# Delta-rule stage: PSUM evictions moved to ScalarE, square roots by logarithm, engine queues tied to the recorded TensorE order, and a full-height rotary product

## The chip, the cores and the metric

The kernel runs on one core of a Trainium2 chip. The metric is device time in microseconds (us), the median of the runs; the profile is of one further execution. Engines are called as on the profile's page: PE (TensorE), PEld (its weight loads), DVE (VectorE), ACT (ScalarE), POOL (GpSimd), SP (SyncE, which issues the DMAs).

## What is computed

One layer of a gated encoder on two sequences (512 and 256 tokens, joined to 768 columns), width 2048. A wide input projection feeds two branches: a gated delta rule over 8 heads of 128 in both directions, and a latent attention over 8 heads. The two are gated, mixed and projected back. Cut to what matters here:

```
qkv = silu(depthwise_conv(proj_qkv));  q, k = l2norm(q), l2norm(k)          # 8 heads of 128
for each chunk (delta rule, forward and on the reversed sequence):
    a   = I + strict_lower((beta k) k^T * decay);   u, w = a^-1 [beta v, beta k exp(g)]
    v'  = u - w S;   o = (q exp(g)) S + lower(q k^T * decay) v'
    S   = S exp(g_last) + (k exp(g_last - g))^T v'
o_a = rmsnorm(o_fwd + o_bwd) * silu(gate_a)
o_b = softmax((q_nope k_nope^T + rot(q_pe) rot(k_pe)^T) / sqrt(192)) v * silu(gate_b)
y   = rmsnorm(x + (sigmoid(gm_a) * (o_a w_pa) + sigmoid(gm_b) * (o_b w_pb)) w_out)
```

Products that need precision are made of three products of halves: each float32 operand is split into a rounded high part and a low part, and high*high, high*low and low*high are summed in PSUM.

## The kernel before

A Python class records the program instruction by instruction. The order of PE's instructions is written out by a little clock: a main generator yields after each projection product, and tasks (generators that `spawn` starts) yield the model nanoseconds after which they want to go on; `run` lets a due task record its next piece between two products. A task's `yield 4000` therefore means "go on once PE has been given 4 us more of work, by the model's prices". PE keeps the recorded order. The queues of DVE, ACT and POOL are then made by the compiler's scheduler, which simulates the engines and puts an instruction into its engine's queue where its inputs are ready in that simulation. Each queue runs strictly in order on the chip. `here_on` ties one instruction behind the latest PE instruction recorded so far, without a semaphore.

The work has three phases. Phase 1 (to about 1400 us) is the input projection: first by a seven-product scheme (`seven`), which fills PE, then nine ordinary blocks (`OTHERS`, columns of `gm_b`), each scaled on DVE, put through a sigmoid on ACT and stored. Phase 2 is the latent projections, phase 3 the two branch projections and the output projection. Between the products of the nine ordinary blocks and of phase 2, about 1240 to 1800 us, the delta rule's tasks run, one head after the other, with the next head begun before the last one is done:

- `gdn_decays` makes the decay matrices E of a head: POOL multiplies masks with gates (`rh`), PE sums them, ACT takes exp, POOL masks. Four groups per head; the first three heads are made ahead.
- `gdn_front` turns k to tokens (`ktok`, PE transposes and a DVE copy), ACT sums squares (`ss`), DVE makes `cc`, PE makes k k^T and q^T k (`kq`), DVE makes U from them, ACT `qk`.
- `gdn_values` does the same sums for q, takes square roots (`sk`, `rq`), and scales the transposed v (`vs`).
- `gdn_blocks` inverts the 32 by 32 diagonal blocks on DVE: 31 steps of two instructions (`spare`, `Y`), then a transpose into `spare`. `gdn_place` copies the result into X and W, half of the copies on ACT, half on DVE.
- `gdn_merge` joins blocks in small PE products with evictions between them (`q1s`, X and W, `q2s`, X).
- `gdn_chain`, four at a time (two sequences, two directions), walks the chunks: PE, then `r` (DVE) and `t` (ACT), PE, then `vn`, PE, then the state S, E (ACT) and an addition (POOL).
- `gdn_end` adds the directions, sums squares on ACT (`junk`, `so`), takes the root, inverts it into `f`, and scales.

Four PSUM buffers (`aps`) serve all of these, and the scores of attention too. On ACT a function that the loaded table set lacks is preceded by an `ACT_TABLE_LOAD`.

In attention the rotary part of the scores uses `qpe`, whose first 64 rows hold the high part and whose last 64 the low part, and `kpe[0]` and `kpe[1]`, the high and low part of the rotated keys, the same in both halves of the rows.

Of the kernel before, what the change touches and what calls it, by code (L numbers as in the profile page):

```python
# [53 lines left out]

class Layer:
# [4 lines left out]
    def __init__(self, tc, a):  # L60
        self.tc, self.nc, self.a = tc, tc.nc, a
        self.es = ExitStack()
# [573 lines left out]
    def gdn_decays(self, s):  # L636

        nc, gp, h = self.nc, self.gp, s["h"]
        E = s["E"] = gp.tile([P, 2, NCH, P], F32, name="E", bufs=3)
        for d in range(2):  # L640
            mask = self.minc[d].unsqueeze(1).broadcast_to([P, 3, P])
            for g0 in (0, 3):
                parts = []
                for src in (self.ghi, self.glo):
                    rh = gp.tile([P, 3, P], F32R, name="rh", tag="rh", bufs=3)
                    nc.gpsimd.tensor_tensor(rh, mask, src[:, g0:g0 + 3, d * 8 + h].bitcast(F32).unsqueeze(2).broadcast_to([P, 3, P]), op=ALU.mult)
                    parts.append(rh)
                yield 4000
                ps = self.apsum()
                for i in range(2):  # L650
# [7 lines left out]
    def gdn_front(self, s):  # L658
        nc, gp, h, kq = self.nc, self.gp, s["h"], s["kq"]
# [4 lines left out]
        for c0, n, ps in self.tposed(kT):  # L664
            nc.vector.tensor_copy(ktok[:, c0:c0 + n, :], ps)
# [27 lines left out]
    def gdn_values(self, s):  # L693

        nc, gp = self.nc, self.gp
# [6 lines left out]
        nc.scalar.activation(sk, ss, AF.Sqrt, bias=self.eps)  # L702
        s["rq"] = small("rq", [NCH])
        nc.vector.reciprocal(s["rq"], sk[:, 1, :])
# [10 lines left out]
    def gdn_blocks(self, s):  # L715


        nc, gp = self.nc, self.gp
# [26 lines left out]
    def gdn_place(self, s, R):  # L745

        nc, X, W = self.nc, self.X, self.W
# [11 lines left out]
    def gdn_merge(self, s, d):  # L759

        nc, gp, U, X, W = self.nc, self.gp, s["U"][:, d], self.X[d], self.W[d]
# [20 lines left out]
        for p in range(2):  # L782
            A, B = src(p), dst(p)
            nc.vector.tensor_scalar(X[A, :, B], x1[A, :192].rearrange("p (n c) -> p n c", c=32), -1.0, None, op0=ALU.mult)
            if p == d:
                nc.vector.tensor_scalar(W[B, :, wc], x1[B, 192:384].rearrange("p (n c) -> p n c", c=32), -1.0, None, op0=ALU.mult)
# [6 lines left out]
        nc.vector.tensor_copy(q2s[B], q2[B, :384].rearrange("p (n c) -> p n c", c=64))  # L793
# [4 lines left out]
        nc.vector.tensor_scalar(X[A, :, B], x2[A, :384].rearrange("p (n c) -> p n c", c=64), -1.0, None, op0=ALU.mult)  # L798
# [6 lines left out]
    def gdn_chain(self, s, q, d):  # L805
        nc, gp, h, o = self.nc, self.gp, s["h"], s["E"][:, d]
        chunks = SEQS[q] if d == 0 else SEQS[q][::-1]
        S = None
        for step, n in enumerate(chunks):
# [16 lines left out]
            nc.vector.tensor_scalar(vn, p2[:, 0:P], s["cc" if first else "ncc"][:, d, n:n + 1], None, op0=ALU.mult)  # L826
# [8 lines left out]
            if not last:  # L835
                new = gp.tile([P, P], F32, name=f"S{q}{d}", bufs=2 - q)
                if first:
                    nc.vector.tensor_copy(new, p3[:, P:2 * P])
# [12 lines left out]

    def gdn_end(self, s):
        nc, gp = self.nc, self.gp
# [8 lines left out]
        nc.scalar.activation(so, so, AF.Sqrt, bias=self.eps, scale=1.0 / P)  # L862
        f = gp.tile([P, NCH], F32, name="f", bufs=2)
        nc.vector.reciprocal(f, so)
# [64 lines left out]
    def phase1(self):  # L929
# [16 lines left out]
        for i, t in enumerate(OTHERS):  # L946
# [3 lines left out]
            nc.scalar.activation(f, f, AF.Sigmoid)  # L950
# [130 lines left out]
    def attention(self):  # L1081
# [20 lines left out]
        def scores(u):  # L1102
# [3 lines left out]
            for i in range(2):  # L1106
# [4 lines left out]
                self.mm(s, qpe[h][:64, qs], kpe[1][:64, keys], start=False, stop=True)  # L1111
# [74 lines left out]
    def phase3(self):  # L1186
# [47 lines left out]
        def mixed(j, i, g, pa):  # L1234
            def done(f):
                x = raws[j][i]
                nc.vector.tensor_tensor(g, f, g, op=ALU.mult)
# [304 lines left out]
```

## Time and profile before

| | |
|---|---|
| median of 3 runs (lowest, highest) | 2547.22 us (2547.01, 2550.58) |
| the profiled execution | 2548.74 us |
| its span, first to last instruction | 2547.0 us |
| PE busy | 2430.3 us (95%) |
| DVE busy | 1960.1 us (77%) |
| ACT busy | 1112.6 us (44%) |
| POOL busy | 539.1 us (21%) |
| mean granted clock of PE | 0.975 of full speed |

A busy PE means that a matmul was in flight; matmuls overlap, so the distance from one start to the next is shorter than one matmul's duration. The page's 40 slices show PE at nine tenths or more nearly everywhere; the lower digits stand at the start, from about 1280 to 1730 us, around 2110 to 2310 us and in the last slice. The granted clock is below nine tenths in slices near 1300, and near the end.

### The profile page before, as it was taken

The numbers are of one execution on the slowest core, as the hardware profiler recorded it, in microseconds if no ns is written. First come the engines' busy times: TensorE is split into PE (matmuls) and PEld (weight loads), VectorE is DVE, ScalarE is ACT, GpSimd is POOL, SyncE is SP. The second block draws the span as 40 slices with busy tenths as digits, with TensorE's granted clock in tenths as the row PEclk, the third lists the DMA queues.
The fourth block names the chain that finished last, engine by engine and source line by source line (L and its number), as shares of the span: only waits on it lengthen the run. The fifth ranks groups of instructions, "written<-read, shape, count | busy, mean of one in ns | idle before, by whom it ended". The sixth has DMA issues, their size and how long they took to land. (4 is left out here: it accounts for less than half of the span.)

```text
span 2547.0 us, 41374 instructions
## 1 busy us (share of the span) xinstructions
PE 2430.3 (95%) x15062; PEld 2303.9 (90%) x15062; DVE 1960.1 (77%) x4294; ACT 1112.6 (44%) x2337; POOL 539.1 (21%) x456
## 2 busy tenths in 40 slices
PE   7999999999999999999989999989999999979997
PEld 6999999999999999999978878878888788968997
DVE  8777888888888887777458899888344567988876
ACT  6553343333333343334526665444344543334442
POOL 5210000000000000000734444443443331032112
PEclk9999999999999999999979999999999999989998
DMA  5542223233222232223312253322375444533346
GB/s 178 180 159 85 102 96 105 97 108 103 97 98 98 96 118 98 98 98 119 125 46 78 77 175 127 119 87 82 114 234 172 137 159 148 176 102 123 130 161 217
DMA packets 157564, 313.45 MB, mean 123 GB/s; under 512 B 17072, under 2 KB 35888, under 8 KB 157360
## 3 DMA queue, kind: packets, MB, share of 16 engines
q1 hardware_dynamic: 157360, 310.81, 36.8%
q8 instruction: 118, 1.93, 0.3%
q14 instruction: 86, 0.70, 0.1%
HBM read 236.33 MB, written 72.45 MB: 121 GB/s over the span
## 5 line engine op out<-in xcount | busy, mean ns | idle before, releaser
L198 ACT CAST Thi<-T 128x512 fp32r<-128x512 f32 x400 | 247.5, 619 | 660.2 <-PE P L86 286.7
L200 DVE TENSOR_TENSOR Tlo<-T,Thi 128x512 fp32r<-128x512 f32 x400 | 284.1, 710 | 225.8 <-ACT Thi L198 221.9
L458 POOL TENSOR_TENSOR wlo<-wraw,whi 128x512 fp32r<-128x512 f32 x113 | 154.3, 1367 | 1179.2 <-ACT whi L453 1124.0
L194 DVE TENSOR_TENSOR T<-wraw,T 128x128 f32<-128x128 f32 x800 | 261.1, 327 | 14.0
L199 DVE TENSOR_TENSOR wlo<-wraw,whi 128x384 fp32r<-128x384 f32 x400 | 227.1, 568 | 0.3 <-ACT whi L191 0.2
L191 ACT CAST whi<-wraw 128x384 fp32r<-128x384 f32 x400 | 203.2, 508 | 39.0 <-PE P L86 31.1
L194 DVE TENSOR_TENSOR T<-wraw 128x256 f32<-128x256 f32 x400 | 169.5, 424 | 9.3 <-DMA wraw<-in_w_pb 6.7
L453 ACT CAST whi<-wraw 128x512 fp32r<-128x512 f32 x130 | 79.9, 617 | 108.5 <-PE ps L86 87.9
L573 DVE SCALAR_TENSOR_TENSOR f<-pad,cols,f 128x772 f32<-128x772 f32 x96 | 97.2, 1012 | 0.1
L736 DVE TENSOR_TENSOR spare<-Y,V 128x126 f32<-128x126 f32 (+22 forms) x248 | 92.0, 371 | 4.8
L738 DVE TENSOR_TENSOR Y<-Y,spare 128x126 f32<-128x126 f32 (+22 forms) x248 | 88.7, 358 | 4.7
L86 PE MATMUL ps<-ch,wlo 128*128 128x512 f32 (+1 forms) x288 | 79.0, 353 | 0.0
L86 PE MATMUL ps<-cl,whi 128*128 128x512 f32 (+1 forms) x288 | 78.7, 351 | 0.0
L86 PE MATMUL ps<-ch,whi 128*128 128x512 f32 (+1 forms) x288 | 78.4, 351 | 0.0
L86 PE MATMUL P<-mS,Thi 128*128 128x384 f32 x224 | 76.4, 343 | 0.7 <-ACT s L230 0.6
L86 PE MATMUL ps<-oah,whi 128*128 128x512 f32 (+1 forms) x256 | 68.4, 345 | 1.6 <-DVE g L1198 1.6
L896 POOL TENSOR_TENSOR acc<-acc,f 128x768 f32<-128x768 f32 x13 | 24.9, 1917 | 206.0 <-DVE wlo L199 131.7
L86 PE MATMUL ps<-oal,whi 128*128 128x512 f32 (+1 forms) x256 | 68.2, 345 | 0.0
L86 PE MATMUL ps<-oah,wlo 128*128 128x512 f32 (+1 forms) x256 | 68.0, 345 | 0.0
L223 DVE TENSOR_TENSOR f<-P,f 128x384 f32<-128x384 f32 x117 | 64.1, 549 | 0.2
L1296 POOL TENSOR_TENSOR rstd<-rstd,x 128x768 f32<-128x768 f32 x13 | 32.8, 2523 | 138.3 <-ACT x L1295 137.9
L1438 POOL TENSOR_TENSOR mX<-R,mH 128x768 fp32r<-128x768 f32 x8 | 30.3, 3782 | 133.0 <-ACT mH L1439 115.5
(779 smaller groups left out, 8158.9 us busy)
## 6 DMA issues: line engine op xcount, KB each, us to landing
wraw<-in_w_in SPq DMA_DIRECT2D x356, 256.0 KB, 2.7
wraw<-in_w_out SPq DMA_DIRECT2D x64, 256.0 KB, 2.7
wraw<-in_w_pa SPq DMA_DIRECT2D x32, 256.0 KB, 3.5
wraw<-in_w_pb SPq DMA_DIRECT2D x32, 256.0 KB, 3.8
xa<-in_xT SPq DMA_DIRECT2D x16, 384.0 KB, 3.7
xtok<-in_x SPq DMA_DIRECT2D x24, 256.0 KB, 3.7
qkv_d<-f SPq DMA_DIRECT2D x24, 256.0 KB, 2.0
sma_d<-f SPq DMA_DIRECT2D x16, 384.0 KB, 2.5
```

The costliest lines, as they stand in the source:

```text
L86: ins = self.nc.tensor.matmul(out, lhsT, rhs, start=start, stop=stop, **kw)
L191: nc.scalar.copy(hi[:, 1:], raw[:, 1:])
L194: tt = lambda o, x, y: self.after_floor(nc.vector.tensor_tensor(o, x, y, op=ALU.add))
L198: nc.scalar.copy(thi, t)
L199: first = nc.vector.tensor_tensor(lo[:, 1:], raw[:, 1:], hi[:, 1:].bitcast(F32), op=ALU.subtract)
L200: last = nc.vector.tensor_tensor(tlo, t, thi.bitcast(F32), op=ALU.subtract)
L223: add = lambda out, a, b, op=ALU.add: nc.vector.tensor_tensor(out, a, b, op=op)
L453: copy = nc.scalar.copy(hi, raw)
L458: eng.tensor_tensor(lo, raw, hi.bitcast(F32), op=ALU.subtract)
L573: nc.vector.scalar_tensor_tensor(acc, pad[:, k:k + 772], w[:, ct, k:k + 1], acc, op0=ALU.mult, op1=ALU.add)
L736: nc.vector.tensor_tensor(tmp[:, :a, :w], Y[:, :a, j:j + 1].broadcast_to([P, a, w]), V[:, j:j + 1, j + 1:].broadcast_to([P, a, w]), op=ALU ...
L738: nc.vector.tensor_tensor(Y[:, :a, j + 1:], Y[:, :a, j + 1:], tmp[:, :a, :w], op=ALU.subtract)
```

## The change

1. `Ordered`, a wrapper over the engines. In all delta-rule functions each DVE, ACT and POOL instruction is tied by `here_on` behind the PE instruction recorded last.
2. Evictions of one source go from DVE to ACT: `ktok`, the negated X and W and `q2s` of `gdn_merge`, `vn`, and the first state S of a chain.
3. The two square roots of a head (for `sk`/`rq` and for `f`) become exp(-0.5 ln x) on ACT with one Newton step on POOL (`inverse_root`); the DVE reciprocals of both go away.
4. The four groups of `gdn_decays` are 9000 model ns apart instead of 4000, but for head 0.
5. The sigmoid of the nine ordinary blocks moves from phase 1 to phase 3, to where the stored block has been loaded again (`mixed`).
6. The last rotary product of the scores uses all 128 rows of `qpe` and `kpe[1]`, where it used 64. It adds low*low to the sum.

```diff
+class Ordered:
+    def __getattr__(self, name):
+        x = getattr(self.of, name)
+        if name in ("vector", "scalar", "gpsimd"):
+            return Ordered(self.layer, x)
...
+        def call(*args, **kw):
+            ins = x(*args, **kw)
+            self.layer.here_on(ins)
+            return ins
+        return call
...
-                yield 4000
+                yield 4000 if h == 0 else 9000
...
-            nc.vector.tensor_copy(ktok[:, c0:c0 + n, :], ps)
+            nc.scalar.copy(ktok[:, c0:c0 + n, :], ps)
...
-        nc.scalar.activation(sk, ss, AF.Sqrt, bias=self.eps)
-        s["rq"] = small("rq", [NCH])
-        nc.vector.reciprocal(s["rq"], sk[:, 1, :])
+        rr = small("rr", [2, NCH])
+        nc.gpsimd.tensor_scalar(ss, ss, EPS, None, op0=ALU.add)
+        self.inverse_root(rr, ss, sk)
+        s["rq"] = rr[:, 1]
+        nc.gpsimd.tensor_tensor(sk[:, 0], ss[:, 0], rr[:, 0], op=ALU.mult)
...
-            nc.vector.tensor_scalar(X[A, :, B], x1[A, :192].rearrange("p (n c) -> p n c", c=32), -1.0, None, op0=ALU.mult)
+            nc.scalar.mul(X[A, :, B], x1[A, :192].rearrange("p (n c) -> p n c", c=32), -1.0)
...
-        nc.vector.tensor_copy(q2s[B], q2[B, :384].rearrange("p (n c) -> p n c", c=64))
+        nc.scalar.copy(q2s[B], q2[B, :384].rearrange("p (n c) -> p n c", c=64))
...
-            nc.vector.tensor_scalar(vn, p2[:, 0:P], s["cc" if first else "ncc"][:, d, n:n + 1], None, op0=ALU.mult)
+            nc.scalar.mul(vn, p2[:, 0:P], s["cc" if first else "ncc"][:, d, n:n + 1])
...
+    def inverse_root(self, y, x, t):
+        nc = self.onc
+        nc.scalar.activation(y, x, AF.Ln)
+        nc.scalar.activation(y, y, AF.Exp, scale=-0.5)
+        nc.gpsimd.tensor_tensor(t, y, y, op=ALU.mult)
+        nc.gpsimd.tensor_tensor(t, t, x, op=ALU.mult)
+        nc.gpsimd.tensor_scalar(t, t, -0.5, 1.5, op0=ALU.mult, op1=ALU.add)
+        nc.gpsimd.tensor_tensor(y, y, t, op=ALU.mult)
...
-        nc.scalar.activation(so, so, AF.Sqrt, bias=self.eps, scale=1.0 / P)
-        nc.vector.reciprocal(f, so)
+        nc.gpsimd.tensor_scalar(so, so, 1.0 / P, EPS, op0=ALU.mult, op1=ALU.add)
+        self.inverse_root(f, so, junk[:, :NCH])
...
-            nc.scalar.activation(f, f, AF.Sigmoid)
...
-                self.mm(s, qpe[h][:64, qs], kpe[1][:64, keys], start=False, stop=True)
+                self.mm(s, qpe[h][:, qs], kpe[1][:, keys], start=False, stop=True)
...
+                if 72 + j + 8 * i in OTHERS:
+                    nc.scalar.activation(g, g, AF.Sigmoid)
                 nc.vector.tensor_tensor(g, f, g, op=ALU.mult)
```

PE's order changes little: the merge of each head stands at the same place among the projection products within 8 of them. What moves is on the other queues. In the rows below L453 (before) and L474 (changed) are the casts of projection weights, L69 (changed) is the wrapper's line, under which all delta-rule instructions now stand.

ACT, first head, from the root of `gdn_values` to the placing copies (X and W from `spare`). Before:

```order
L702 ACTIVATE sk<-ss,eps 128x12
L453 CAST whi<-wraw 128x512
L653 ACT_TABLE_LOAD
L653 ACTIVATE E<-aps 128x384
L453 CAST whi<-wraw 128x512
L653 ACTIVATE E<-aps 128x384
L754 COPY X_12973<-spare 32x6x32
L754 COPY W_12974<-spare 32x6x32
L754 COPY X_12973<-spare 32x6x32
L453 CAST whi<-wraw 128x512
```

Now:

```order
L69 ACT_TABLE_LOAD
L69 ACTIVATE rr<-ss 128x12
L69 ACT_TABLE_LOAD
L69 ACTIVATE rr<-rr 128x12
L474 CAST whi<-wraw 128x512 x2
L69 ACTIVATE E<-aps 128x384
L474 CAST whi<-wraw 128x512 x3
L69 COPY X_12973<-spare 32x6x32
L69 COPY W_12974<-spare 32x6x32
L69 COPY X_12973<-spare 32x6x32
```

Between the root and the first placing copy there were two weight casts, and there are five now; the root takes a table load for Ln and one for Exp.

DVE, second chain step of the first head beside the next head's inversion (`spare`, `Y`). Before:

```order
L819 SCALAR_TENSOR_TENSOR r_14035<-aps,ex,vs 128x128
L736 TENSOR_TENSOR spare<-Y,V 128x31
L479 TENSOR_TENSOR evt<-ps,rstd 128x768
L738 TENSOR_TENSOR Y<-Y,spare 128x31
L826 TENSOR_SCALAR vn_14085<-aps,ncc 128x128
L736 TENSOR_TENSOR spare<-Y,V 128x30
L826 TENSOR_SCALAR vn_14091<-aps,ncc 128x128
L738 TENSOR_TENSOR Y<-Y,spare 128x30
L826 TENSOR_SCALAR vn_14097<-aps,ncc 128x128
L736 TENSOR_TENSOR spare<-Y,V 128x2x29
L826 TENSOR_SCALAR vn_14105<-aps,ncc 128x128
```

Now:

```order
L69 SCALAR_TENSOR_TENSOR r_14037<-aps,ex,vs 128x128
L69 TENSOR_TENSOR spare<-Y,V 128x31
L69 TENSOR_TENSOR Y<-Y,spare 128x31
L69 TENSOR_TENSOR spare<-Y,V 128x30
L69 TENSOR_TENSOR Y<-Y,spare 128x30
L69 TENSOR_TENSOR spare<-Y,V 128x2x29
L69 TENSOR_TENSOR Y<-Y,spare 128x2x29
```

The four `vn` have left the queue; the inversion's steps follow each other.

ACT, end of the second head (`junk`, then the root into `f`) beside the next head's front. Before:

```order
L861 ACTIVATE junk,so<-E,rqs 128x128 x3
L453 CAST whi<-wraw 128x512
L862 ACT_TABLE_LOAD
L862 ACTIVATE so<-so,eps 128x6
L667 ACTIVATE aps,ss<-aps 128x128 x5
L773 COPY q1s<-aps 32x192
L667 ACTIVATE aps,ss<-aps 128x128
L773 COPY q1s<-aps 32x192 x3
```

Now:

```order
L69 ACTIVATE junk,so<-E,rqs 128x128
L474 CAST whi<-wraw 128x512
L69 ACT_TABLE_LOAD
L69 ACTIVATE f<-so 128x6
L69 COPY ktok<-aps 128x512
L69 ACT_TABLE_LOAD
L69 ACTIVATE f<-f 128x6
L69 COPY ktok<-aps 128x256
L69 ACTIVATE aps,ss<-aps 128x128 x5
L69 COPY q1s<-aps 32x192
L69 ACTIVATE aps,ss<-aps 128x128
L69 COPY q1s<-aps 32x192 x3
```

Ahead of `q1s` there are now two table loads, two activations and two `ktok` copies where there were one load and one activation; the `junk` sums stand between the placing copies instead of behind them (not shown).

## Rows read from the trace of the kernel before

**Rows 1.** Stages: from:to, length, busy of PE, PEld, DVE, ACT, POOL, clock, DMA.

```profile
1241.00:1303.00 62.00, 50.70 (x289) 48.95 (x287) 44.14 (x100) 32.36 (x70) 36.39 (x40) 0.94 0.20 66
1303.00:1372.00 69.00, 66.61 (x463) 60.41 (x463) 44.25 (x134) 27.66 (x83) 18.69 (x23) 0.78 0.15 54
1372.00:1792.00 420.00, 387.49 (x3245) 340.67 (x3244) 354.69 (x924) 230.60 (x638) 182.73 (x205) 0.96 0.34 110
1860.00:1992.00 132.00, 132.00 (x739) 108.21 (x739) 65.20 (x135) 63.88 (x124) 48.42 (x30) 1.00 0.60 192
1992.00:2112.00 120.00, 118.75 (x693) 96.67 (x691) 79.60 (x164) 62.25 (x130) 47.18 (x29) 1.00 0.48 158
```

**Rows 2.** Waits of PE from 1280 to 1800 us: total, times, longest.

```profile
PE aps L86 <- POOL rh L646: 9.7, 1, 9.7
PE aps L86 <- ACT t L821: 8.2, 7, 2.2
PE aps L86 <- ACT q1s L773: 4.8, 3, 2.4
...
PE aps L86 <- DVE vn L826: 2.2, 5, 0.9
```

**Rows 3.** Timeline of all engines around the longest wait: start, duration, instruction, [idle before].

```profile
1295.45 0.71 DVE L741 STREAM_TRANSPOSE spare<-Y 128x512 f32<-128x512 f32 x1
...
1296.19 0.51 ACT L754 COPY X<-spare 32x192 f32<-32x192 f32 x1 [14.96 <-DVE spare L741]
...
1298.37 1.27 POOL L458 TENSOR_TENSOR wlo<-wraw,whi 128x512 fp32r<-128x512 f32 x1 [14.88 <-ACT whi L453]
...
1301.78 0.69 PE L86 MATMUL aps<-rh,mr 128*128 128x384 f32 x1 [9.75 <-POOL rh L646]
```

**Rows 4.** Timeline of DVE: one step of the inversion beside POOL, one without.

```profile
1268.05 1.21 DVE L738 TENSOR_TENSOR Y<-Y,spare 128x30 f32<-128x30 f32 x1
...
1289.15 0.28 DVE L738 TENSOR_TENSOR Y<-Y,spare 128x120 f32<-128x120 f32 x1
```

**Rows 5.** Groups of DVE: busy us, mean ns of one, idle before and its releaser.

```profile
L826 DVE TENSOR_SCALAR vn<-aps,ncc 128x128 f32<-128x128 f32 x64 | 21.5, 341 | 4.7 <-PE aps L86 4.7
L784 DVE TENSOR_SCALAR X<-aps 32x192 f32<-32x192 f32 x32 | 11.3, 353 | 14.1 <-PE aps L86 13.5
L793 DVE COPY q2s<-aps 64x384 f32<-64x384 f32 x16 | 8.8, 552 | 14.2 <-PE aps L86 14.0
...
L864 DVE RECIPROCAL f<-so 128x6 f32<-128x6 f32 x8 | 1.5, 191 | 13.0 <-ACT so L862 12.9
```

**Rows 6.** Groups of ACT.

```profile
L821 ACT ACTIVATE t<-aps,ex 128x128 f32<-128x128 f32 x64 | 22.6, 367 | 39.3 <-DVE r L819 38.6 <-POOL E L844 0.3
L773 ACT COPY q1s<-aps 32x192 f32<-32x192 f32 x32 | 9.9, 308 | 2.2 <-PE aps L86 1.6
L862 ACT ACT_TABLE_LOAD x6 | 7.7, 1283 | 0.1
L950 ACT ACTIVATE evt<-evt 128x768 f32<-128x768 f32 x9 | 7.6, 845 | 1.6 <-DVE evt L479 1.5
L558 ACT ACT_TABLE_LOAD x1 | 1.3, 1283 | 0.0
```

**Rows 7.** Groups of POOL.

```profile
L844 POOL TENSOR_TENSOR E<-E,t 128x128 f32<-128x128 f32 x64 | 31.7, 506 | 64.0 <-ACT E L842 63.9
L723 POOL MEMSET PK<- 128x256 f32 x8 | 2.5, 312 | 12.5 <-DVE W L757 9.1 <-ACT aps L667 3.3
```

**Rows 8.** Timeline of PE, end of one block of scores, looked at in narrow windows.

```profile
1872.75 0.63 PE L86 MATMUL aps<-L,L 128*128 128x512 f32 x2
...
1872.98 0.83 PE L86 MATMUL aps<-L,L 128*128 128x512 f32 x2
...
1873.31 0.50 PE L86 MATMUL aps<-L,L 64*128 64x512 f32 x1
...
1873.73 0.50 PE L86 MATMUL ps<-oal,whi 128*128 128x512 f32 x1
```

More of the change, by code (lines that the diff above doesn't have):

```diff
@@ L52, with __init__ @@
 PAIRS = order()
+class Ordered:
+    def __init__(self, layer, of):
+        self.layer, self.of = layer, of
+    def __getattr__(self, name):
+        x = getattr(self.of, name)
+        if name in ("vector", "scalar", "gpsimd"):
+            return Ordered(self.layer, x)
+        if self.of is self.layer.nc:
+            return x
+        def call(*args, **kw):
[3 more added lines that the diff above has]
+        return call
 class Layer:
@@ L61, in __init__ @@
         self.tc, self.nc, self.a = tc, tc.nc, a
+        self.onc = Ordered(self, self.nc)
         self.es = ExitStack()
@@ L636, in gdn_decays @@
     def gdn_decays(self, s):
-        nc, gp, h = self.nc, self.gp, s["h"]
+        nc, gp, h = self.onc, self.gp, s["h"]
         E = s["E"] = gp.tile([P, 2, NCH, P], F32, name="E", bufs=3)
@@ L658, in gdn_front @@
     def gdn_front(self, s):
-        nc, gp, h, kq = self.nc, self.gp, s["h"], s["kq"]
+        nc, gp, h, kq = self.onc, self.gp, s["h"], s["kq"]
         small = lambda name, sh: gp.tile([P] + sh, F32, name=name, bufs=2)
@@ L693, in gdn_values @@
     def gdn_values(self, s):
-        nc, gp = self.nc, self.gp
+        nc, gp = self.onc, self.gp
         small = lambda name, sh: gp.tile([P] + sh, F32, name=name, bufs=2)
@@ L715, in gdn_blocks @@
     def gdn_blocks(self, s):
-        nc, gp = self.nc, self.gp
+        nc, gp = self.onc, self.gp
         U, X, W, V = s["U"], self.X, self.W, self.V
@@ L745, in gdn_place @@
     def gdn_place(self, s, R):
-        nc, X, W = self.nc, self.X, self.W
+        nc, X, W = self.onc, self.X, self.W
         cols = [R[:, :, 0:24].rearrange("p a (g d n) -> p d n a g", g=2, d=2)[:, d] for d in range(2)]
@@ L759, in gdn_merge @@
     def gdn_merge(self, s, d):
-        nc, gp, U, X, W = self.nc, self.gp, s["U"][:, d], self.X[d], self.W[d]
+        nc, gp, U, X, W = self.onc, self.gp, s["U"][:, d], self.X[d], self.W[d]
         src = lambda p: slice(64 * p + 32 * d, 64 * p + 32 * d + 32)
@@ L783, in gdn_merge @@
             A, B = src(p), dst(p)
-            nc.vector.tensor_scalar(X[A, :, B], x1[A, :192].rearrange("p (n c) -> p n c", c=32), -1.0, None, op0=ALU.mult)
+            nc.scalar.mul(X[A, :, B], x1[A, :192].rearrange("p (n c) -> p n c", c=32), -1.0)
             if p == d:
-                nc.vector.tensor_scalar(W[B, :, wc], x1[B, 192:384].rearrange("p (n c) -> p n c", c=32), -1.0, None, op0=ALU.mult)
+                nc.scalar.mul(W[B, :, wc], x1[B, 192:384].rearrange("p (n c) -> p n c", c=32), -1.0)
         yield 2600
@@ L797, in gdn_merge @@
             self.mm(x2[A, 64 * n:64 * n + 64], q2s[B, n, :], X[B, n, B], start=True, stop=True, tile_position=(B.start, A.start))
-        nc.vector.tensor_scalar(X[A, :, B], x2[A, :384].rearrange("p (n c) -> p n c", c=64), -1.0, None, op0=ALU.mult)
+        nc.scalar.mul(X[A, :, B], x2[A, :384].rearrange("p (n c) -> p n c", c=64), -1.0)
         s["merged"] += 1
@@ L805, in gdn_chain @@
     def gdn_chain(self, s, q, d):
-        nc, gp, h, o = self.nc, self.gp, s["h"], s["E"][:, d]
+        nc, gp, h, o = self.onc, self.gp, s["h"], s["E"][:, d]
         chunks = SEQS[q] if d == 0 else SEQS[q][::-1]
@@ L837, in gdn_chain @@
                 if first:
-                    nc.vector.tensor_copy(new, p3[:, P:2 * P])
+                    nc.scalar.copy(new, p3[:, P:2 * P])
                 else:
@@ L850, in gdn_chain @@
             s["done"] = True
+    def inverse_root(self, y, x, t):
[6 more added lines that the diff above has]
+        nc.gpsimd.tensor_tensor(y, y, t, op=ALU.mult)
     def gdn_end(self, s):
-        nc, gp = self.nc, self.gp
+        nc, gp = self.onc, self.gp
         o = [s["E"][:, d] for d in range(2)]
```

## The prediction

> **What bounds the kernel now.** I read the stages first. From 128 to 1150 us PE is never idle on the page's 40 slices and the change does not reach there. It reaches three places: the delta rule (about 1241 to 1792 us), attention (about 1860 to 2060 us), and, by the nine sigmoids, the mixing stage from 2110 us. In the delta rule PE is busy but not always: it idles 11.3 of the 62 us of the first head's first half, 2.4 of the next 69, and 32.5 of the 420 us of the other heads [rows 1]. The next 69 us hide a second loss: the granted clock is 0.78 there, so 69 x 0.22 = 15 us are lost to the lower of the two levels (1.2 GHz in place of 2.4) although PE looks busy; the 420 us lose 420 x 0.04 = 17 us in the same way [rows 1]. So 46 us of idle time and 32 us of clock are all that any change on the other engines can win here. DVE is the fullest of the others, 354.7 of 420 us (84%), ACT stands at 230.6 (55%) [rows 1]. In attention PE is busy the whole 132 us from 1860, at full clock [rows 1]: there PE's own work is the time.
>
> Then the waits. The longest by far is one of 9.7 us [rows 2], and the timeline tells its chain backwards: PE waits for POOL's `rh`, POOL for a weight cast of ACT (14.88 us), ACT for the placing copy that heads its queue and needs the inversion's last transpose (14.96 us) [rows 3]. Nothing PE needed just then depended on the inversion; it stood behind it in a queue. The other PE waits are small: 8.2 us for `t`, 4.8 for `q1s`, 2.2 for `vn` [rows 2]; `t` itself waits 38.6 us for DVE's `r` over the run [rows 6].
>
> **The rotary product.** In a block of scores two 128-row matmuls start 0.23 us apart (1872.75, 1872.98), the 64-row one 0.33 us after its predecessor (1873.31), and the next product 0.42 us after that (1873.73) [rows 8]. Against two distances of 0.23 that is 0.75 - 0.46 = 0.29 us more per block. Blocks: 8 heads x 3 units x 2 = 48, so 14 us if each is on the path. From 1860 to 1992 us PE has no idle time, so about half of them (four of eight heads, 24) count fully, 7 us. The rest run where PE has 1.25 of 120 us idle [rows 1] but attention is its own chain of scores, softmax and transposes; I credit them with 0.2 us, 5 us. Together **-12 us**, bounds -7 and -14.
>
> **The first head.** The built order puts three more weight casts ahead of the placing copies, so PE is fed until it reaches the small merge products by itself. How far is that? PE stalled at about 1292 us (1301.78 less 9.75) [rows 3]. By the order 36 projection matmuls stand between this place and the merge; at 50.70 us for 289 matmuls, 0.175 us each in this stretch [rows 1], PE arrives at about 1298. The inversion's transpose ends at 1296.16 and six placing copies of 0.51 end at 1299.2 [rows 3]. So some 1 us of the wait stays, exposed at a new place, and the merge starts near 1299.5 where it now starts after 1301.78 plus two groups: 3 us from the copies and about 3 more from the load of the sigmoid's table and its activation, which leave this stretch. **-5 us**, bounds -9 and 0 (0 if the inversion ends later). The wider spacing of the decays works in the same place: a step of the inversion takes 1.21 us beside POOL and 0.28 without [rows 4], and POOL has fewer `rh` and masks to make while the first inversion runs; I take it as cover for the added POOL work of the roots, 0 net.
>
> With a wait of 1 us in place of 9.7 the clock need not fall. Its 15 us [rows 1] are the larger prize, but the low clock lies over the small merge products, whose evictions would set the pace at full clock; I take half, **-7 us**, bounds -15 and 0.
>
> **The other heads.** From DVE go: 96 `vn` of 341 ns (32.7 us), 48 X and W of 353 ns (16.9), 32 of the 64x384 form of `q2s` at 552 ns (17.7), which is 67 us, and 48 copies `ktok` and S; the reciprocals of both roots are 16 x 0.19 = 3 us [rows 5]. Some 9 us per head of the 70 that one head takes. ACT gets the same instructions: `vn` at the 367 ns of `t` (35.2 us), X and W at the 308 ns of `q1s` (14.8), the 64x384 form between 308 and DVE's own 552, say 430 (13.8) [rows 5, 6]. So the sum moves and does not shrink, and the two engines end level near 70%. In a chain step this is a gain: `vn` no longer stands between inversion steps. I credit half of the waits for `vn` and `t`, and some of the idle time that the view gives no engine for, **-8 us**.
>
> In the merge it is a loss. There ACT already makes the placing copies, the `junk` sums and the root ahead of `q1s`, for which PE waits 4.8 us [rows 2]. Now `ktok`, X, W and `q2s` come on top, and the root grows: before, one table load (1.283), one activation (0.3, as `q1s`) and the reciprocal (0.191), 1.77 us; now two loads and two activations, 3.17 us, and five small POOL instructions. POOL's rows give 0.506 us for a 128x128 addition and 0.312 for a fill of 128x256 [rows 7]; for 6 to 12 elements I take 0.3, nearer the fill, bounds 0.1 and 0.5. That is 4.7 us, 2.9 more per root (bounds 1.9 and 3.9). DVE waits for it in order: before its `f` it already idles 13.0 us over the run, all for the root [rows 5], and behind `f` stand `cc` and the twelve U of the next head, whose `aps` buffers PE needs. I let a third of 8 x 2.9 reach PE, **+8 us**, bounds 0 and +31. The heads' net is then 0.
>
> Do the roots go "without table loads"? Not in the built order: a load before Ln and one before Exp, 32 for 16 roots, where the delta-rule stage had 38 for roots, exps and sigmoids; 6 x 1.283 = 8 us less on ACT, hidden. The trace has this pair once already, in the gates, where Exp behind Ln has a load of its own (L558) [rows 6].
> The Trainium skill ("ScalarE: Activation LUTs", Table sets: the hidden batching unit) says that ln and then exp need one load, since one set holds both. By that each root would cost 1.28 us less; this case's row disagrees, and the sum goes by the row.
> The same page (Rules for kernel authors) advises VectorE, not ScalarE, for adds and multiplications. This trace shows 341 ns on DVE against 367 on ACT for 128x128 out of PSUM [rows 5, 6]; by either the move costs ACT about what it frees on DVE, and it pays only where DVE's queue is the later one.
>
> **The sigmoids.** Nine of 845 ns [rows 6] leave the first stretch and come back in the mixing stage, once each between the load of a block and its product on DVE. They wait for no matmul, but PE does lose time in this stage to evictions on ACT. **+1 us**, bounds 0 and +4; if a sigmoid headed the queue while its block was still loading, the weight casts behind it would wait.
>
> **Sum**: -12 - 5 - 7 - 8 + 8 + 1 = -23 us against the profiled execution's 2548.7, which is its span of 2547.0 and 1.7 around it: 2525.7. That execution lies 1.5 us over the median of the runs shown, so 2524 us.
>
> **Rivals.**
> *ACT becomes the bound of the merge.* For it: two loads, `ktok` and three more evictions ahead of the chain, in a queue that PE already waits on. Against it: the first head's wait goes by order alone. Then only the rotary product and the first 5 us stay, and the heads lose 7: 2547.2 - 12 - 5 + 7 + 1 = 2538.
> *The waits were mostly queue order.* For it: the 9.7 us wait and the 38.6 us of `t` behind `r`. Then half of the 46 us idle and 25 of the 32 us of clock go besides the 14 of the rotary product: 2547.2 - 23 - 25 - 14 = 2485.
> *The root heads DVE's queue (slower).* Place: `f` at the end of each head. At the upper price of 3.9 us, plus the `ktok` copy that stands between Ln and Exp and waits for PE (0.6), the next head's U start 4.5 us later, 8 x 4.5 = 36 us, and the lower clock follows the longer waits. It decides once more than 3 us per head reach PE (the other terms bring 25 without the heads' own gain). Time: 2547.2 - 12 + 36 = 2571.
> *One set serves both* (the loads of Exp fall away): 16 x 1.283 = 21 us off ACT, of which by the same third 7 reach PE: 2517. Its ground is the page named above, and the built order speaks against it.
> *Nothing to measure*: 2547, if the rotary product's gain is lost behind attention's chain and the heads level out.
>
> **How the numbers follow.** Forecast 0.48 (2508 to 2535), ACT-bound merge 0.22, mostly order 0.15, slower 0.09, one set 0.03, nothing 0.03. A measurement of this kernel can tell 0.2%, 5 us. Faster: 0.48 + 0.22 + 0.15 + 0.03, less 0.02 for the edge of the second case, is 0.86; within: 0.05; slower: 0.09. The range reaches somewhat past the better case's time and past the ACT-bound one, 2481 to 2544, and leaves out the slower case, a third of the better and the flat one, somewhat under 0.2.
>
> **What would show it.** Right: 128-row matmuls at 0.23 us in every block of scores; no wait near 10 us before the first merge; clock near 1 behind it; DVE near 70% in the heads, ACT as well; 32 table loads in the delta rule. Wrong: waits of PE for `q1s`, X or U that grow from 5 us to 20; DVE's idle time before `f` far over 13 us; a low clock in other heads; weight casts on ACT late in the mixing stage.

## The result and the profile after

The changed kernel takes 2573.8 us (median of 4 runs, 2566.3 to 2576.3) against 2547.1 (2539.0 to 2550.6) for the kernel before: a ratio of 1.0104, 95% interval 1.0072 to 1.0137. It is slower by 27 us; the prediction said 23 us faster, 2481 to 2544.

The profiled execution of the changed kernel took 2575.5 us, its span is 2573.7. The page's first block, and its row of the granted clock in 40 slices:

```profile
PE 2436.3 (95%) x15062; PEld 2324.4 (90%) x15062; DVE 1905.3 (74%) x4054; ACT 1168.6 (45%) x2571; POOL 558.3 (22%) x544
...
PEclk9999999999999999999989899989999999989998
```

DVE has 55 us less to do and ACT 56 more: the move happened as described, and the sum did not shrink. The stages tell where the time went. PE's order hardly changed, so the same piece of work can be cut out of both traces: from the first merge product of the second head to the first chain product of the last head, and from the first score product of attention to its last transposed product. First the kernel before, then the changed one (from:to, length, busy of PE, PEld, DVE, ACT, POOL, granted clock, DMA share, GB/s):

```profile
1375.00:1800.00 425.00, 392.49 (x3292) 344.37 (x3291) 355.55 (x925) 228.34 (x632) 182.23 (x203) 0.96 0.34 111
...
1872.00:2068.00 196.00, 195.08 (x1115) 156.88 (x1115) 110.29 (x259) 104.43 (x221) 70.09 (x42) 1.00 0.49 156
```

```profile
1241.00:1299.00 58.00, 52.98 (x309) 52.24 (x308) 36.97 (x91) 20.30 (x55) 32.19 (x38) 1.00 0.23 78
1299.00:1372.00 73.00, 67.45 (x479) 60.92 (x480) 42.17 (x111) 38.38 (x121) 29.61 (x41) 0.84 0.17 56
1372.00:1841.00 469.00, 417.00 (x3291) 365.95 (x3290) 318.55 (x739) 279.38 (x825) 198.55 (x275) 0.90 0.30 99
...
1913.00:2094.00 181.00, 179.22 (x1121) 158.61 (x1120) 109.82 (x260) 101.88 (x220) 70.67 (x42) 1.00 0.52 170
```

- Attention: 196 us became 181 (180.1 to the last product's end), at full clock in both. In a block of scores five 128-row products now leave in 1.15 us, 0.23 us each, where the half-height one used to cost more [rows 8]:

```profile
1913.80 1.31 PE L107 MATMUL aps<-L,L 128*128 128x512 f32 x5
1914.95 0.51 PE L107 MATMUL ps<-oal,whi 128*128 128x512 f32 x2
```

- The first head [rows 1, 3]: the wait of 9.7 us for `rh` is gone, but one of 5.2 us stands in its place, for the placed W (first row: PE's waits from 1241 to 1303, total, times, longest). Before its first placing copy ACT had been idle for 8.38 us, until the inversion's last transpose (`spare`, on DVE) had ended (the rows below: start, duration, instruction, [idle before]):

```profile
PE aps L107 <- ACT W L69: 6.2, 2, 5.2
```

```profile
1298.21 0.51 ACT L69 COPY X<-spare 32x192 f32<-32x192 f32 x1 [8.38 <-DVE spare L69]
...
1299.19 0.84 PE L107 MATMUL aps<-W,U 32*32 32x32 f32 x12 [5.21 <-ACT W L69]
```

- The other heads: 425 us became 469, for the same 3290 matmuls. PE's idle time grew from 32.5 to 52.0 us, and its *busy* time from 392.5 to 417.0, because the granted clock fell from 0.96 to 0.90. So a little under half of the loss is waiting and the rest is slow work. PE's waits in these 469 us (`ACT aps` is a PSUM buffer that ACT's squares still hold); [rows 2] has the waits of before:

```profile
PE aps L107 <- ACT E L69: 10.2, 8, 2.5
PE aps L107 <- DVE r L69: 8.4, 7, 2.3
PE aps L107 <- DVE S L69: 6.8, 6, 3.0
PE aps L107 <- ACT aps L69: 6.7, 5, 3.1
PE aps L107 <- ACT W L69: 4.4, 4, 1.6
...
PE aps L107 <- ACT q1s L69: 3.3, 3, 2.0
```

No single wait stands out, which is why this view alone does not give the cause. The wait for `q1s`, which the prediction had named as a sign, is shorter than before (3.3 us against 4.8); the one for buffers held by ACT's squares grew from 2.2 to 6.7 us, and the one for the copies E of the chains from 1.7 to 10.2. DVE's idle time ahead of `f` did grow as the slower rival said, from 13.0 us [rows 5] to 47.1 (rows on `f`: what its engine waited for, us, times):

```profile
  POOL f L69: 47.1, 8
```

The prices that the prediction had estimated came out near: `vn` 364 ns on ACT, X 321, the 64x384 `q2s` 473, a small POOL instruction 0.20 us; and each root loads a table twice, 32 loads of 1283 ns.

```profile
L69 ACT ACT_TABLE_LOAD x32 | 41.1, 1283 | 0.6
...
L69 ACT ACTIVATE vn<-aps,ncc 128x128 f32<-128x128 f32 x64 | 22.5, 364 | 9.3 <-PE aps L107 9.3
...
L69 ACT COPY q2s<-aps 64x384 f32<-64x384 f32 x16 | 7.6, 473 | 24.9 <-PE aps L107 24.9
```

### The profile page after: what moved, and what is told of

Read it like the earlier page. It is cut to its first block, busy times and chain, and to the rows that moved or that the text cites. A ratio compares the mean times of both kernels' runs of the same rounds, so it can differ in the third digit from the quotient of the medians.

```text
span 2573.7 us, 41491 instructions
## 1 busy us (share of the span) xinstructions
PE 2436.3 (95%) x15062; PEld 2324.4 (90%) x15062; DVE 1905.3 (74%) x4054; ACT 1168.6 (45%) x2571; POOL 558.3 (22%) x544
## 5 line engine op out<-in xcount | busy, mean ns | idle before, releaser
L474 ACT CAST whi<-wraw 128x512 fp32r<-128x512 f32 x130 | 79.8, 619 | 82.1 <-PE ps L107 60.9
L69 DVE TENSOR_TENSOR Y<-Y,spare 128x126 f32<-128x126 f32 (+22 forms) x248 | 93.4, 376 | 7.2
L69 DVE TENSOR_TENSOR spare<-Y,V 128x126 f32<-128x126 f32 (+22 forms) x248 | 94.1, 380 | 6.2
L69 DVE SCALAR_TENSOR_TENSOR U<-aps,cc,E 128x128 f32<-128x128 f32 x96 | 27.3, 344 | 54.2 <-PE aps L107 54.0
```

The source lines that it names most:

```text
L69: ins = x(*args, **kw)
L474: copy = nc.scalar.copy(hi, raw)
```

## The experiments

Each run was timed beside the kernel before. Differences between runs are taken from the ratios, times 2547 us, since the runs come from several groups. An interval reaches 4 to 8 us to either side, so the difference of two runs is uncertain by some 5 to 10 us.

| kernel | median us | ratio to before (95%) |
|---|---|---|
| rotary product alone | 2531.4 | 0.9951 (0.9936, 0.9966) |
| changed, no tied order | 2561.4 | 1.0056 (1.0037, 1.0075) |
| changed, old roots | 2532.4 | 0.9949 (0.9934, 0.9964) |
| changed, evictions on DVE | 2576.0 | 1.0131 (1.0105, 1.0158) |
| changed, old root at `f` only | 2541.9 | 0.9989 (0.9970, 1.0007) |
| changed, scaling by `f` on POOL | 2577.7 | 1.0119 (1.0104, 1.0134) |
| changed, no Newton step at `f` | 2576.1 | 1.0096 (1.0067, 1.0125) |
| changed, Sqrt and POOL steps at `f` | 2544.3 | 0.9981 (0.9967, 0.9995) |
| changed, root of `f` later | 2576.0 | 1.0108 (1.0092, 1.0125) |
| changed, filling matmuls | 2564.1 | 1.0069 (1.0050, 1.0089) |
| old roots, filling matmuls | 2534.5 | 0.9949 (0.9934, 0.9964) |
| old roots, merge evictions on DVE | 2542.3 | 0.9983 (0.9966, 0.9999) |
| **old roots, no tied order** | **2518.3** | **0.9890 (0.9865, 0.9915)** |
| old roots, decays 4000 apart | 2523.1 | 0.9900 (0.9875, 0.9925) |
| old roots, sigmoids back | 2534.6 | 0.9945 (0.9926, 0.9965) |
| old roots, `vn` and S on DVE | 2534.8 | 0.9947 (0.9928, 0.9967) |
| old roots, no tied order, decays 4000 | 2528.1 | 0.9911 (0.9879, 0.9943) |
| the same, all evictions on DVE | 2531.9 | 0.9941 (0.9918, 0.9963) |

### Which part: rotary, order, roots, evictions

Edits: the rotary line alone in the kernel before; `self.onc = self.nc` in the changed one; the old root lines put back; the seven evictions put back on `nc.vector`.

```diff
-        self.onc = Ordered(self, self.nc)
+        self.onc = self.nc
```

> The kernel before with the 128-row rotary product and nothing else. In the changed kernel the stretch from the first score product to the last transposed product of attention is 16 us shorter than before (180.2 against 196.1). If that is the product's own gain, this run gives 2547 - 15 = 2532 us, between 2530 and 2534, under each of the three theories on the delta rule. If the 16 us came instead from attention beginning later, with its operands ready earlier, this run stays within 5 us of 2547.

> The changed kernel with the wrapper switched off: DVE, ACT and POOL queues of the delta rule are again in the order that the scheduler's simulation gives. Theory Q (the tied queue order is what costs the later heads some 45 us): 2530 to 2540. Theory R (the longer roots at the head of DVE's queue): 2565 to 2578, since the roots stay. Theory A (the evictions crowd ACT): 2565 to 2578 as well.

> The changed kernel with the old roots: Sqrt on ACT and the reciprocal on DVE in both places, all else as changed. Theory R: the loss of 45 us in heads two to eight goes for the most part, 2530 to 2545. Theories Q and A: 2565 to 2575.

> The changed kernel with the seven kinds of evictions (ktok, X and W, q2s, the second X, vn, the first S) back on DVE, the rest as changed. Theory A: 2530 to 2545. Theory R: 2570 or more, since the fuller DVE waits for the root just the same. Theory Q: 2565 to 2580.

The rotary product gives 12.5 us by its ratio (9 to 16), and its attention stretch is the 180 us of the changed kernel: that part is settled. The roots are the loss: with the old ones the time is 2532, 39 us less by the ratios. The evictions show no clear difference in this company (2576; 7 us by the ratios, and the intervals overlap). The tied order costs 12 us, give or take 10. The same stretch of the heads with the old roots is back at 432 us:

```profile
1367.60:1799.50 431.90, 396.07 (x3287) 350.69 (x3287) 318.60 (x753) 269.09 (x807) 181.81 (x204) 0.94 0.34 108
```

### By what way the root costs: DVE's wait, POOL's steps or ACT's loads

The old root at `f` alone; the scaling on POOL:

```diff
-        nc.vector.tensor_tensor(f, f, rq, op=ALU.mult)
-        nc.vector.tensor_tensor(o[0], o[0], f.unsqueeze(2).broadcast_to([P, NCH, P]), op=ALU.mult)
+        nc.gpsimd.tensor_tensor(f, f, rq, op=ALU.mult)
+        nc.gpsimd.tensor_tensor(o[0], o[0], f.unsqueeze(2).broadcast_to([P, NCH, P]), op=ALU.mult)
```

no Newton step at `f`:

```diff
-        self.inverse_root(f, so, junk[:, :NCH])
+        nc.scalar.activation(f, so, AF.Ln)
+        nc.scalar.activation(f, f, AF.Exp, scale=-0.5)
```

and Sqrt with POOL steps at `f`:

```diff
-        self.inverse_root(f, so, junk[:, :NCH])
+        nc.scalar.activation(f, so, AF.Sqrt)
+        t = junk[:, :NCH]
+        nc.gpsimd.tensor_tensor(t, f, f, op=ALU.mult)
+        nc.gpsimd.tensor_tensor(t, t, so, op=ALU.mult)
+        nc.gpsimd.tensor_scalar(t, t, 0.0, 1.0, op0=ALU.mult, op1=ALU.add)
+        nc.gpsimd.tensor_tensor(f, f, t, op=ALU.mult)
+        nc.vector.reciprocal(f, f)
```

> The changed kernel with the old root at f alone (Sqrt on ACT, reciprocal on DVE); the root of gdn_values keeps the new form. Theory D (DVE stands at f while the root goes through ACT and POOL, and the next head's cc and U stand behind it) and theory L (the second table load and what stands between Ln and Exp hold back q1s, which is behind them in ACT's queue) both say 2532 to 2545. Theory V (the root of gdn_values, for which vs waits, is the costly one): 2565 to 2575.

> The changed kernel with the two operations behind the root (f times rqs, E times f) on POOL in place of DVE. ACT's queue, PE's order and the root are unchanged, but DVE no longer waits for it. Theory D: 2535 to 2550. Theory L: 2570 to 2580, nothing is won.

> The changed kernel without the four POOL instructions of the Newton step at f; Ln, Exp and both table loads stay. f comes some 1.1 us earlier per head (four instructions of 0.2 us and the passages between them). The root is a little less exact. Theory D: 8 x 1.1 us and some of the lower clock, 2555 to 2566. Theory L: 2570 to 2576.

> The changed kernel with one table load and one activation (Sqrt) at f, then four POOL instructions of the same kind as the Newton step (they multiply by one), then the reciprocal on DVE. Against the old root at f alone the chain to f is longer by some 1.2 us, ACT's queue is the same. Theory D: 2543 to 2555, some 10 us above the run with the old root at f. Theory L: within 4 us of that run.

Theory D, DVE at the head of its queue, which is the prediction's own slower rival, falls three times. With the scaling on POOL, DVE waits for no root at all and the time stays (2578). Without the Newton step `f` comes earlier and the time stays (2576). With one load and a longer way through POOL the time is that of the old root at `f` (2544 against 2542). And DVE's wait ahead of U was no shorter without the wait at `f`: it is for PE, 58.4 us against 54.2 in the changed kernel. The row is of the kernel with the scaling on POOL:

```profile
L69 DVE SCALAR_TENSOR_TENSOR U<-aps,cc,E 128x128 f32<-128x128 f32 x96 | 27.3, 344 | 58.4 <-PE aps L107 58.3
```

What is left is ACT's queue. The merge of the second head shows it, since up to there both queues are alike. The changed kernel, ACT and PE (start, duration, instruction, [idle before]):

```profile
1376.49 1.28 ACT L69 ACT_TABLE_LOAD   x1
...
1377.78 0.21 ACT L69 ACTIVATE f<-so 128x6 f32<-128x6 f32 x1
...
1378.01 0.31 ACT L69 COPY q1s<-aps 32x192 f32<-32x192 f32 x1
1378.34 1.28 ACT L69 ACT_TABLE_LOAD   x1
1379.63 0.21 ACT L69 ACTIVATE f<-f 128x6 f32<-128x6 f32 x1
1379.87 0.31 ACT L69 COPY q1s<-aps 32x192 f32<-32x192 f32 x1
...
1380.23 0.21 PE L107 MATMUL aps<-X,q1s 32*32 32x32 f32 x1 [2.05 <-ACT q1s L69]
```

and the kernel with Sqrt and POOL steps, the same place:

```profile
1377.45 0.21 ACT L69 ACTIVATE f<-so 128x6 f32<-128x6 f32 x1
...
1377.68 0.63 ACT L69 COPY q1s<-aps 32x192 f32<-32x192 f32 x2
...
1378.37 0.21 PE L107 MATMUL aps<-X,q1s 32*32 32x32 f32 x1 [0.52 <-ACT q1s L69]
```

The second load and Exp stand between the two `q1s`, and PE waits 2.05 us in place of 0.52. In this merge that is the direct price, 1.5 us. But the chain's first product starts 27.3 us after the merge's first in the changed kernel (1372.30 to 1399.62) and 21.1 after it in the other (1371.96 to 1393.06): 6.2 us. The rest is mostly the clock. The changed kernel in pieces of 2 us:

```profile
1378.00:1380.00 2.00, 0.18 (x2) 0.00 (x0) 0.00 (x0) 1.93 (x4) 0.01 (x1) 1.00 0.32 110
1380.00:1382.00 2.00, 1.77 (x38) 1.24 (x38) 0.83 (x2) 1.98 (x11) 0.79 (x4) 0.74 0.06 22
1382.00:1384.00 2.00, 1.78 (x5) 1.18 (x4) 1.07 (x5) 1.92 (x11) 0.00 (x0) 0.50 0.00 0
...
1388.00:1390.00 2.00, 2.00 (x10) 1.61 (x9) 0.00 (x0) 1.35 (x3) 0.42 (x1) 0.50 0.00 0
1390.00:1392.00 2.00, 2.00 (x16) 1.64 (x14) 1.36 (x5) 0.17 (x2) 2.00 (x4) 0.70 0.00 0
```

PE is idle for nearly the whole of 1378 to 1380, and from about 1381 to 1391 it works at the lower level, though it is busy again from 1382 on; in the other kernel the clock reads 1.00 in every piece of this merge. The four `kq` products take 2.08 us here and 1.13 there.

One merge proves little: the kernel before and the one with the rotary product alone share their delta rule, and their second merges took 20.8 us (clock 1.00) and 26.5 us (0.74). So here are the merges of heads two to eight and the chain stretches between them, summed over one profiled execution each:

| kernel | merges, us | PE idle in them, us | chain stretches, us |
|---|---|---|---|
| before | 151.0 | 8.9 | 273.8 |
| changed | 181.5 | 18.4 | 287.1 |
| Sqrt and POOL steps at `f` | 152.3 | 12.2 | 287.2 |
| old root at `f` only | 157.6 | 12.6 | 287.4 |
| old roots | 154.0 | 11.3 | 277.9 |

The other three kernels with the new root at `f` under the tied order (evictions on DVE, scaling on POOL, no Newton step) have 180.7 to 190.3 us of merges. So the root at `f` costs in the merges, some 29 us, of which 6 are idle time and 23 are PE's work at a lower clock. What PE waits for there differs from merge to merge: `q1s` in the one shown, in three others a buffer that the squares hold (1.8, 1.4 and 3.1 us), for the squares too stand behind both loads in ACT's queue.

The root of `gdn_values` costs too: 2541.9 with it new against 2532.4 with both old, 10 us by the ratios. By the table it lies in the chains, 287 us against 278. Its two loads stand ahead of the copies of S and E there, in the changed kernel for instance:

```profile
1407.14 1.28 ACT L69 ACT_TABLE_LOAD   x1
1408.44 0.21 ACT L69 ACTIVATE rr<-rr 128x12 f32<-128x12 f32 x1
1408.56 0.25 ACT L69 COPY E<-aps 128x128 f32<-128x128 f32 x1
...
1408.86 0.60 PE L107 MATMUL aps<-S,kq 128*128 128x128 f32 x3 [2.22 <-ACT E L69]
```

PE's waits for E, 10.2 us in the changed kernel and 12.4 with the old root at `f` only, are absent with both roots old.

### Whether the place or the load, and whether the clock

```diff
+        yield 12000
         f = gp.tile([P, NCH], F32, name="f", bufs=2)
...
-        yield 12000
+        yield 4000
...
+    def fill(self, ps, want):
+        for _ in range(6 * want):
+            self.nc.tensor.matmul(ps[:, 384:512], self.ident, self.ident, start=True, stop=True)
```

> The changed kernel with the root of f recorded 12 us (of the model's clock) later: in ACT's queue its two loads and two activations then stand behind q1s and the first X and W of the next head's merge, in most heads still ahead of the last q2s and X. The instructions are the same. If their place ahead of q1s is what makes them costly: PE's wait for q1s goes, part of it comes back at q2s, 2545 to 2562. If it is ACT's load as such, wherever it lies in the head: 2568 to 2578.

> The changed kernel with 12 matmuls of 128x128 per head that compute nothing of use (identity by identity, into unused columns), six where PE waits for the placed W of the first merge and six where it waits for q1s. They take 8 x 12 x 0.21 = 20 us of PE at full clock, most of it within waits (18 us in the merges of heads two to eight). Theory C (the low clock after these waits, 38 us in the merges of heads two to eight, is the larger half of the loss, and it comes from PE standing idle there): the clock stays near full in the merges, 2540 to 2560. If the low clock comes from the small 32x32 products or from chance: 2575 to 2595, the added work is paid in full.

> The same 12 filling matmuls per head in the changed kernel with the old roots (2532 without them, with 15 us of low clock in the merges of heads two to eight and 12 in the first). Theory C: 2510 to 2530. Otherwise 2535 to 2550.

> The changed kernel with the old roots, and the evictions of the front and merge (ktok, X, W, q2s, second X) back on DVE; vn and the first S stay on ACT. The prediction charged these evictions together with the root to ACT's queue ahead of q1s. If they cost anything there: 2522 to 2529, faster than the 2532 of the old roots alone. If ACT has room for them once the root is short: within 4 us of 2532.

The first hunk is the later root (the transposes behind it then follow after 4 us in place of 12), the second the filling. The later root won nothing (2576), so the place ahead of `q1s` alone is not the answer. No wait for `q1s` is left among the first rows of PE's waits, but others came in its place. The three shown are for work that ACT or the later root now delivers late (1368 to 1835 us, in the slowest of its four executions, 2586 us):

```profile
PE aps L112 <- DVE E L69: 12.9, 5, 4.5
PE aps L107 <- ACT W L69: 10.1, 6, 3.1
...
PE aps L107 <- ACT kd L69: 5.3, 3, 2.4
```

The filling matmuls settle the clock. The same stretch of the heads, first the changed kernel with them, then the kernel with the old roots and them:

```profile
1367.80:1825.80 458.00, 411.12 (x3455) 366.17 (x3455) 316.77 (x738) 279.41 (x824) 197.86 (x275) 0.97 0.31 101
```

```profile
1364.50:1798.70 434.20, 401.91 (x3455) 356.43 (x3455) 318.23 (x753) 269.60 (x807) 180.61 (x204) 0.99 0.33 107
```

With PE occupied in two waits of each merge the clock stands at 0.97 in place of 0.90, and at 0.99 in place of 0.94. The changed kernel gets some 9 us faster (give or take 10) although PE does an estimated 20 us of useless work; with the old roots the work and the clock cancel (2534.5 against 2532.4). The small products are the same in both, so in these runs the low clock goes with the idle time in the merges, not with the small products as such. It is the larger half of the loss in the heads; but filling is no cure: with the old roots it costs what it saves.

Evictions of front and merge on DVE, with the old roots: 2542, 9 us slower, the intervals apart. Once the root is short, their move to ACT is a gain, under the tied order.

### What took the other gains back

With the old roots the changed kernel is as fast as the rotary product alone, though it should also have had the first head's gain and the evictions'. Each remaining part was taken out of it; the last two runs took out several.

```diff
-                yield 4000 if h == 0 else 9000
+                yield 4000
```

> The changed kernel with the old roots (2532) and without the tied queue order. With the new roots the tied order cost 12 us (2574 against 2561). If it does so with the old ones as well, it is the part that takes the first head's gain back: 2518 to 2526. If it only cost there because it put the two loads ahead of q1s: 2530 to 2540.

> The changed kernel with the old roots and the decays of all heads 4000 model ns apart, as before. The prediction held the wider spacing for cover of POOL's added work, worth 0: within 4 us of 2532. If the wider spacing holds up the later heads: 2520 to 2528. If it spares the merges a clash of POOL with DVE: 2537 to 2545.

> The changed kernel with the old roots and the nine sigmoids back in phase 1, each with a table load of its own and one more for the exp or root behind it. By the theory that a table load among the delta rule's evictions costs more than its 1.28 us: 2540 to 2555. The prediction gave the move +1 in the mixing stage and 3 of the first head's 5 us: 2534 to 2537.

> The changed kernel with the old roots and vn and the first S back on DVE. The prediction gave their move a gain of 8 us: 2538 to 2542. If ACT is the later queue in the chains now, their return to DVE wins: 2520 to 2528.

> The old roots, no tied order, decays 4000 model ns apart; evictions on ACT, sigmoids late and the rotary product stay. If the two losses add up: 2532 - 14 - 9 = 2509, between 2505 and 2514. If they are one and the same clash in the merges: 2516 to 2522, as without the tied order alone.

> As the run beside it, with all seven kinds of evictions back on DVE: of the change only the rotary product and the late sigmoids are left. If the evictions on ACT are worth about 10 us (as the front's and merge's were under the tied order): 2526 to 2532. If they are worth nothing: within 4 us of the run beside it.

The tied order costs 15 us with the old roots as well, and the wider decays 12, each give or take 7. The stretch of the heads without the tied order:

```profile
1358.90:1785.40 426.50, 389.24 (x3287) 341.93 (x3287) 307.73 (x747) 268.33 (x795) 183.45 (x203) 0.97 0.34 109
```

Its clock is 0.97 in place of 0.94, its idle time the same (37 us against 36), and the heads begin earlier: the first merge at 1293.8 us in place of 1297.7. From 1241 to 1850 us PE waits 10.8 us for the placed W with the tied order (first row), 3.9 without it (second):

```profile
PE aps L107 <- ACT W L69: 10.8, 6, 5.2
```

```profile
PE aps L107 <- ACT W L775: 3.9, 2, 2.6
```

Of the 10.8 us, 6.3 stand at the first head, where there is no `junk` of an earlier head yet and ACT waits for the inversion; without the tied order the whole 3.9 stands there. The 4.5 us of the later heads are gone without it. They are the queue that front and prediction had noted without a price: with the tied order the `junk` sums, which wait for the last additions of the head before, stand between the placing copies on ACT, and in the second head PE waits 2.3 us for W behind them.

The sigmoids are worth nothing either way: put back, they bring 13 more table loads to ACT (50 in the trace in place of 37) and the time is 2534.6 against 2532.4. So a load has no fixed price: what counts is what PE waits for behind it. `vn` and S: 2534.8, no difference.

The two losses do not add up in the time. Both taken out should have given some 2506 us; it is 2528, with runs from 2517.4 to 2533.3 and an interval that reaches over those of either alone. The profiled executions, one each and all with the old roots, show where:

| kernel | 1241 us to the first chain product, us | heads two to eight, us | PE's waits from 1241 to 1306 us |
|---|---|---|---|
| both kept | 84.7 | 431.9 | W 6.3 |
| no tied order | 74.3 | 426.5 | W 3.9 |
| decays 4000 apart | 83.5 | 425.0 | W 9.7, `rh` 1.1 |
| neither | 94.0 | 417.7 | `rh` 11.8 |

Between the two columns lie 41 to 44 us in all four. In heads two to eight the losses do add. The first head takes it back: it is the wider spacing that had shortened PE's long wait there, and without it the wait is back, for W under the tied order and for `rh` without. The last kernel's execution, the slowest of its five, then ran the first merge at a granted clock of 0.51 over 30 us; with all evictions on DVE besides, the same wait was followed by 22.6 us at 0.71, so a part of this is chance. That kernel gives 2531.9, and the intervals overlap: what the evictions are worth without the tied order stays open.

The fastest kernel by its median is the changed one with the old roots and without the tied order: 2518.3 us, 1.1% under the kernel before and 2.1% under the changed one. The one with the old roots and the decays 4000 apart (2523.1) can't be told from it: the intervals overlap.

## Why the prediction was wrong

- **Rotary product, -12 (bounds -7 and -14).** Right: 12.5 us alone. The stretch is 16 us shorter, so both halves lay on the path, and the caution about the second half was not needed.
- **First head, -5 and -7.** The direction was right; the size was not, and the order of the queues was not the reason. The wait of 9.7 us became 5.2 (6.2 in all), not 1: PE was at the merge at 1294.0 (1299.19 less 5.21), not at 1298, and the inversion's transpose ended at 1298.2, not at 1296.2. ACT stood idle for it, so nothing in ACT's queue was in the way. Nor does the wait go "by order alone": with the tied order and the old spacing PE still waits 9.7 us for W. The wider spacing, which the prediction set at 0, is what shortens it. The 3 us credited to the sigmoids that leave did not show either: the first merge starts at 1297.0 us with them back and at 1297.7 without, both with the old roots. The first chain product came 5.7 us earlier (1327.4 against 1333.1) although the stage had begun 3.3 us later. Of the 15 us of low clock behind the wait half was to go; 12 are left (0.84 over 73 us). This low clock is not the wait's alone: with the rotary product alone the first merge took 22.6 us in place of 30.1, with the same delta rule.
- **Other heads, -8 and +8.** Here it failed. The step was "I let a third of 8 x 2.9 reach PE, +8": the root was carried along DVE's queue (`f`, then `cc` and U), and a third was a guess. The runs showed another way, through ACT's queue: the loads with Ln and Exp stand ahead of work that PE waits for, at `f` ahead of `q1s` and the squares of the merge (29 us in the merges), at the root of `gdn_values` ahead of E in the chains (9 us). Together the roots cost 39 us (give or take 9), where the bound was 31. At `f` the POOL instructions, which were a good part of the 2.9, cost nothing that shows, and DVE's wait cost nothing.
- **The size.** The direct price was well within what was written: 1.5 us in the merge shown, some 6 us of idle time over the seven merges. What was missing is that PE's own work then runs at the lower level, for some 10 us in the merge shown. The prediction treated the 17 us of low clock in the heads as something to be won back, not as a price that each new wait adds to. For the whole change that made some 3 us of new idle time per head into 6 of time, 44 us in the stretch, where the heads' net had been put at 0.
- **Two parts had no price.** The tied order was argued only from the first head, and there, with the wider spacing, it makes PE's wait longer (6.3 us against 3.9); in all it costs 12 to 15 us. The wider decays were set at 0 "as cover"; with the old roots they cost 12 under the tied order, although they shorten the first head's wait.
- **Evictions.** "The sum moves and does not shrink" was right, and -8 for the chains was too much: `vn` and S are worth nothing measurable. The front's and merge's, charged as a loss, are a gain of 9 with the old roots under the tied order.
- **Sigmoids, +1.** No difference; right.
- **The table loads.** The built order's two loads per root were right. The Trainium skill ("ScalarE: Activation LUTs", Table sets: the hidden batching unit) has Ln and Exp in one set, by which the second load would not be there; the trace has 32 loads of 1283 ns for 16 roots. With one load and one activation at `f` in place of two and two, the time falls by 29 us.
- **The rivals.** The slower one gave 2571, near the 2574 measured, but that is luck, for it came by a way that did not happen: DVE's wait at `f` did grow (47.1 us) and nobody lost by it. (Its threshold counted 25 us from the other terms; they add up to 23.) "ACT becomes the bound of the merge" had the queue right and the price, 7 us, wrong. Nothing in the profile of before spoke against it strongly enough for 0.22: PE already waited there, 4.8 us for `q1s` [rows 2]. Of the prediction's signs of being wrong two came, DVE's wait ahead of `f` and the low clock in the other heads; the waits for `q1s` did not grow.

## What to carry to other kernels

An engine's average (ACT at 55%) says nothing about a queue that the busiest engine waits on piece by piece; ask what stands ahead of each instruction it waits for, and what the new ones add there. Price a new wait of PE by what it does to the granted clock behind it, not by its own length. And a long wait of another engine, like DVE's at `f`, may be free: move that wait elsewhere before believing that it costs.

## What was not expected of the hardware

- Some 2 us without matmuls were followed by about 10 us at a granted clock of 0.50, with PE busy most of that time; 0.5 us in the same place were not. Occupying PE with products of no use brought the clock from 0.90 to 0.97 over 460 us.
- Executions of one kernel beside each other differ by up to 17 us (2538.0 to 2555.1 us with the old root at `f` only), and the same instructions of the first merge took 30.1 us in one profiled execution (the kernel before) and 22.6 in another (the rotary product alone). One profiled execution is a weak ground for a claim about a few us of clock.
- The price of a table load depends on its place: 13 more with the sigmoids cost nothing that can be measured, while the changed kernel, with 45 loads against 41 for the one with the old root at `f` alone, is 29 us slower. The kernel before has 51 and is 27 us faster than the changed one.
